# Reordering casts, low parts and sums on ScalarE and VectorE in a hybrid decoder layer

## The chip, the cores and the metric

The kernel runs on one core of a Trainium2 chip. The metric is the device time of one execution in microseconds (us), lower is better. The engines are named as in the profile: PE (TensorE, matmuls), DVE (VectorE), ACT (ScalarE), POOL (GpSimd) and SP (SyncE, which here only issues DMAs). Each engine runs its own instructions in order and waits for others through semaphores.

## The reference

One decoder layer on a sequence of 512 tokens with 1024 channels, all in float32:

```
u = rms_norm(x);  proj = u @ w_in                      # q | k | v | GLU inputs | two gates
q = rms_norm(q)*hd**-0.5;  k = rms_norm(k)             # 16 query heads, 4 key/value heads, hd 64
attn = sliding_window_attention(q, k, v, sinks, bias) @ w_attn_o     # window 128, blocks of 128
conv = silu(layer_norm(depthwise_conv31(a*sigmoid(gate)) + b)) @ w_conv_out
x = x + (sigmoid(gate_a)*attn + sigmoid(gate_c)*conv) @ w_out
x = x + square(relu(rms_norm(x) @ w_ff1)) @ w_ff2      # 4096 hidden channels
```

## The kernel before, in words

**Precision by pieces.** Each float32 matrix is split into a high part (a cast to fp32r, on ScalarE) and a low part (the difference, by a subtraction on VectorE or GpSimd). Each product is three matmuls: high by high, high by low, low by high. A "piece" is one such pair, 128x1024 elements: a 1.0 us cast and a 1.2 us subtraction on VectorE (2.4 us on GpSimd).

**Order written out by hand.** The program is a list of events. `at(pos, fn, args)` puts a step at a position; one unit is about a quarter of a 128x512 output tile, and all events run sorted by position. So the positions fix the order of the instructions on PE, ACT, DVE and POOL. Two steps that share no engine do not care about their mutual order; two that do are executed as listed, and the first that has to wait holds the second. SP's transfers and POOL's are issued in the place of their events too, when what they overwrite has been read.

**Attention part (positions 0 to 152).** TensorE computes the GLU tiles h0 to h7 and the query groups q0 to q3 (order h0 h1 q0 h2 q1 h3 q2 h4 h5 q3 h6 h7), and then the gate tiles, one weight piece per tile, with three buffers each for the high and low parts. A weight piece `u` is split (`split_hi` on ScalarE, `split_lo` on GpSimd) just behind the end of use `u-3`; the raw chunk's buffer is reloaded by `load` after the last split of the chunk. For query group g: `q_step` makes the raw queries, `heads_raw` copies them and squares them on ScalarE, `q_sum` reduces the squares on VectorE, `q_root` and `q_scale` on GpSimd normalise, `q_hi` casts on ScalarE, `q_lo` subtracts on GpSimd, and `q_stage` transposes four times on TensorE (`qtp`, L569) into PSUM and copies on ScalarE (`qT`, L570). In between run the attention units (group g, token block t), six positions apart, starting at `u0`: `score`, `score_max` (DVE), `score_exp` (ACT, L709), `score_norm` (POOL), later `prob` (transposition), `prob_hi`, `prob_lo`, `value` (two matmuls into `op`), `value_low` (ACT copies the lower half of `op` to `osb`, L747) and `value_sum` (DVE adds both halves into `attnT`, L754). `qtp`, `ptp` and `op` share two PSUM slots under one tag; a new tile takes the slot that is free first in the written order and waits for that slot's readers. The convolution's taps (L800, DVE) fill VectorE throughout; some taps run on ScalarE and GpSimd.

**MLP part (from position M0 = 256).** Both MLP products are done in four parts of 1024 hidden channels, each a phase of the first product (even phases 0, 2, 4, 6) and a phase of the second (odd phases 1, 3, 5, 7), 28 positions long each. A phase is one step of Strassen-like block arithmetic with seven products, numbered 1 to 7; `ORDER` gives 1, 2, 7, 6, 5, 4, 3 for phase 0 and 1, 7, 6, 2, 5, 4, 3 for the others. Products share PSUM banks by role: 1, 6, 5, 3 accumulate on one pair of banks (one bank for each token half t), 7 and 4 on a second, 2 on a third; between products of one pair the running value is copied or added out (`c_copy` L1189 on ScalarE, `c_add` L1192 and `row_add` L1180 on VectorE). A product has two halves h, each with a weight piece of its own (`piece_hi` L1142 on ScalarE, `piece_lo` L1145 on VectorE); four piece buffers rotate. Piece 7h1 below is the second half's piece of product 7. The sums of weight blocks that the scheme needs come from accumulating DMAs: after `piece_lo` of one product has read a block, `fetch_add` (L1121, POOL queue) adds another weight block from HBM onto it, and the next product's piece is cast from the result. For product 7 in odd phases that transfer makes the block of product 6. The activations' operands are made by `op_sum` (DVE, L1218 to L1223), `op_hi` (ACT, L1209) and `op_lo` (DVE, L1213, always 0.75 positions behind `op_hi`); P7, P5 and P4 are those of products 7, 5 and 4.

Positions that matter here: `products` of product j in a phase starts at `p = m + 4*j` with `m = M0 + 28*phase`, `piece_hi` is by default at `s = p - 5.9 + 2*h`, `piece_lo` at `s + 0.75`, the DMA at `s + 0.9`.

Of the kernel before, what the change touches and what calls it, by code (L numbers as in the profile page):

```python
# [8 lines left out]
F32 = mybir.dt.float32  # L9
# [3 lines left out]
ALU = mybir.AluOpType  # L13
# [9 lines left out]
HD = 64  # L23
NQ = 16
NG = 4
# [28 lines left out]
def tile_hybrid_block(  # L54
# [23 lines left out]
    ve, se, ge, pe = nc.vector, nc.scalar, nc.gpsimd, nc.tensor  # L78
# [269 lines left out]
    def at(pos, fn, *args):  # L348
        events.append((pos, len(events), fn, args))
# [71 lines left out]
    uses = []  # L421
    chunks = []
    pieces = {}

    def chunk(name, w, c0):
        chunks.append((name, w, c0))
        return len(chunks) - 1
# [99 lines left out]
    qTs, state = {}, {}  # L527
# [29 lines left out]

    def q_lo(g):
        qs = qTs[g][0]
        ge.tensor_tensor(out=qs[:, :, 1, :], in0=state["qraw", g].rearrange("p t (h d) -> p (t h) d", d=HD),  # L560
                         in1=qs[:, :, 0, :].bitcast(F32), op=ALU.subtract)

    def q_stage(g, h):
        qs = qTs[g][0]
# [31 lines left out]
    def q_group(g):  # L596
        nonlocal b
        cq = chunk(f"q{g}", w_in, 256 * g)
        us_ = [use(cq, j, Q_SHAPE, b, b + 8) for j in range(2)]
        for t in range(NT):  # L600
            for i in range(2):
                at(b + 2 * t + i, q_step, g, us_, t, i)
            at(b + 2 * t + 2.8, q_sum, g, t)
        b += 8
        p = b + (4.9 if g < 2 else 1.5)
        at(p, q_root, g)
        at(p, q_scale, g)
        p = max(p + 4.4, 24 * (g - 1) + 42.2)
        at(p, q_hi, g)
        at(p + 0.9, q_lo, g)  # L610

    for part in "h0 h1 q0 h2 q1 h3 q2 h4 h5 q3 h6 h7".split():
        (glu_tile if part[0] == "h" else q_group)(int(part[1]))
    for name, c0, tag, res in (("ta", GLU_END, "gate", ta), ("tc", GA_END, "kT", tcv)):
        at(b + 3.9, gate_tiles, name, tag, res)
        for m in range(0, KD, 2):
            cw = chunk(f"{name}{m // 2}", w_in, c0 + P * m)
            for j in range(2):
                T_tile(use(cw, j, T_SHAPE, b, b + 4), b, f"{name}_{m + j}", u_h, u_l, gate, res, m + j,
                       late=3.3 if name == "tc" and m + j == 0 else 0.2)  # L620
# [43 lines left out]
    last_of = {}  # L664
    for u, (ch, j, _, b0, b1) in enumerate(uses):
        if u >= 3:
            at(uses[u - 3][4] + 0.25, split_hi, u)
            at(uses[u - 3][4] + 0.4, split_lo, u)
            last_of[ch] = uses[u - 3][4] + 0.45
        else:  # L670
            last_of[ch] = -3
    ring = [ch for ch in range(len(chunks)) if chunks[ch][0] != "q1"]
# [84 lines left out]
    for g in range(NG):  # L757
        if g:
            at(24 * g + 40.3, load_bias, g)
        for h, p in enumerate((34.5, 35.6, 40.5, 41.6) if g else (39.6, 40.4, 41.1, 41.8)):  # L760
            at(24 * g + p, q_stage, g, h)
        for t in range(NT):
            u0 = UNIT0 + 6 * (NT * g + t)
            at(u0 + 1.9, sink, g, t)
            for hp in range(2):
                at(u0 + 2.05 + 0.01 * hp, score, g, t, hp)
                at(u0 + 2.65 + 0.8 * hp, score_max, g, t, hp)
                at(u0 + 3.15 + 0.8 * hp, score_exp, g, t, hp)
            at(u0 + 4.9, score_root, g, t)
            at(u0 + 5.0, score_norm, g, t)  # L770
            for kb in range(t == 0, 2):
                at(u0 + 13.05 + 0.01 * kb, prob, g, t, kb)
                at(u0 + 13.5 + 0.6 * kb, prob_hi, g, t, kb)
                at(u0 + 13.8 + 0.6 * kb, prob_lo, g, t, kb)
            at(u0 + 15.4, value, g, t)
            at(u0 + 16.1, value_low, g, t)
            at(u0 + 16.4, value_sum, g, t)

# [166 lines left out]
    for ct in range(KD):  # L947
        p = E + 11.95 + 1.35 * ct
# [14 lines left out]
    M0 = W0 + 32  # L963
# [104 lines left out]
    for t in range(NT):  # L1068
        at(W0 + 16.1 + 0.5 * t, lambda t=t: residual(t, 0, tl["acc"][t]))
        at(W0 + 16.6 + 0.5 * t, residual_square, t, 0)  # L1070
        e = W0 + 20 + 4 * t
# [5 lines left out]
        for half in range(2):  # L1077
            late = (1.2, 0.2, 0, 0)[t]
# [146 lines left out]
    def operands(x, p):  # L1225

        for key, pos in p.items():
            if key[0] == "S":
                at(pos, op_sum, x, int(key[1]))
            else:  # L1230
                at(pos, op_hi, x, int(key[1]))
                at(pos + 0.75, op_lo, x, int(key[1]))
# [18 lines left out]
    def acc_of(ph, prod, t):  # L1251
# [10 lines left out]
    at(M0 + 26, open_a, "O")  # L1262
    at(M0 + 20, open_a, "S")
    operands("x", {"P1": M0 - 3.4, "P2": M0 - 1.7, "S3": M0 + 4.6, "P7": M0 + 5.1, "S2": M0 + 6.6,
                   "P6": M0 + 7.3, "S1": M0 + 10, "P5": M0 + 11.5, "P4": M0 + 15.2, "S4": M0 + 18.6, "P3": M0 + 19.6})
    for h in range(2):
        at(W0 + 1 + 0.1 * h, fetch, 0, 0, 0, 0, h)
        at(W0 + 1.3 + 0.1 * h, fetch, 0, 1, 0, 1, h)
# [2 lines left out]
    for ph in range(PHASES):  # L1271
        m = M0 + 28 * ph
        order = ORDER[ph]
        ff1 = ph % 2 == 0
        h11, ht, h22, h21 = homes(ph)
        if ff1:
            for h in range(2):
                if ph:
                    q1, q3, q2, q4 = m - 4.3 + 2 * h, m - 3.4 + 2 * h, m - 1.0 + 2 * h, m + 8.8 + 1.2 * h
                else:  # L1280
                    q1, q3, q2, q4 = W0 + 7.3 + 4.6 * h, W0 + 18 + 0.9 * h, m + 5.2 + 1.7 * h, m + 10.2 + 0.9 * h
                at(q1, block_sum, h11, h11, ht, h)
                at(q3, block_sum, ht, ht, h22, h)
                at(q2, block_sum, ht, h11, h22, h)
                if ph:
                    at(q4, block_sum, ht, ht, h21, h)
                else:
                    at(m + 7.4 + 2 * h, fetch_add, ph, ht, 1, 0, h)
                at(q4 + 0.1, fetch, ph + 1, h21, 0, 1, h)
                at(q4 + 5, fetch_add, ph + 1, h21, 1, 1, h)  # L1290
        elif ph + 1 < PHASES:
            for h in range(2):
                at(m + 7 + h, fetch, ph + 1, homes(ph - 1)[2], 0, 0, h)
        for j, prod in enumerate(order):
            p = m + 4 * j
            for h in range(2):
                n = 2 * (7 * ph + j) + h
                s, lo = p - 5.9 + 2 * h, 0.75
                if ph == 0 and j < 2:
                    s, lo = ((W0 + 5.6, 0.75), (W0 + 8.2, 0.75), (W0 + 21.8, 1.1), (W0 + 22.6, 4.5))[n]  # L1300
                elif not ff1 and prod == 7:
                    s = m - 2.95 + 3 * h
                elif not ff1 and prod == 6:
                    s = p - 3.4 + 2 * h
                at(s, piece_hi, n, home(ph, prod), h)
                at(s + lo, piece_lo, n, home(ph, prod), h)
                for t in range(2):
                    at(p + 2 * h + t, products, ph, prod, n, h, t)
                d = s + 0.9
                if ff1:  # L1310
                    if prod == 5:
                        at(d, fetch, ph + 1, h11, 0, 0, h)
                    elif prod == 4:
                        at(d, fetch, ph + 1, ht, 1, 0, h)
                elif prod == 1:
                    at(d, fetch_add, ph, h11, 0, 1, h)
                elif prod == 7:
                    at(d, fetch_add, ph, ht, 0, 0, h)
                elif prod == 6:
                    at(d, fetch_add, ph, ht, 1, 0, h)  # L1320
                elif prod == 2:
                    at(d, fetch, ph, h21, 1, 1, h)
                elif ph + 1 < PHASES:
                    at(d, fetch, ph + 1, home(ph, prod), *{5: (0, 1), 4: (1, 1), 3: (1, 0)}[prod], h)
            for t in range(2):
                e = p + 3.1 + t
                if ff1:
                    if prod in (1, 7, 6):
                        at(e, c_copy, {1: 0, 7: 3, 6: 2}[prod], ph, prod, t)
                    elif prod == 3:  # L1330
                        at(e, relu_of, 1, ph, prod, t, -1.0)
                    else:
                        at(e, c_add, {2: 0, 5: 3, 4: 2}[prod], ph, prod, t)
                else:
                    half_t, half_n, minus, store = {1: (0, 0, 0, 0), 7: (1, 1, 1, 0), 6: (1, 0, 0, 0), 2: (0, 0, 0, 1),
                                                    5: (1, 1, 1, 1), 4: (1, 0, 0, 1), 3: (0, 1, 1, 1)}[prod]
                    at(e, row_add, ph, half_t, half_n, prod, t, minus, store)
            if ff1 and prod in (2, 5, 4):
                i, scale = {2: (0, 1.0), 5: (3, -1.0), 4: (2, 1.0)}[prod]
                late = 7.6 if ph == 0 and prod == 2 else 0  # L1340
                at(p + 4.9 + late, relu, i, scale)
                at(p + 5.5 + late, square_of, i)
            elif ff1 and prod == 3:
                at(p + 4.8, square_of, 1)
        if ff1:
            e = {prod: m + 4 * j + 4 for j, prod in enumerate(order)}
            operands("a", {"P1": m + (18.2 if ph else 20.5), "S3": e[4] + 2.2, "P7": e[4] + 2.9, "S2": e[4] + 4.4, "P6": e[4] + 5.1,
                           "P2": e[3] + 7.5, "S1": e[3] + 9.5, "P5": e[3] + 10.3, "P4": e[3] + 13.2,
                           "S4": e[3] + 16, "P3": e[3] + 17})

# [94 lines left out]
```

## Time and profile before

| | |
|---|---|
| median of 3 runs | 764.76 us (764.54 to 764.77) |
| the profiled execution's own time | 764.11 us |
| its span, first to last instruction | 762.3 us |
| TensorE busy | 752.4 us, 99% (weight loads 663.2) |
| VectorE, ScalarE, GpSimd busy | 603.1 (79%), 439.8 (58%), 275.4 us (36%) |
| DMA | 97.48 MB, mean 128 GB/s |
| granted TensorE clock | 1.000 |

How to read the rows that follow. A timeline row has the start, the duration, the engine, the line, the operation, output<-inputs by tile name, shapes and the count of merged instructions; in brackets at the end stands how long the engine was idle before it and what ended that. A row of the waits has who waited for whom, the total, the number of times and the longest. Matmuls are pipelined, so the duration of one is longer than the step from one start to the next, and a wait costs more than the idle time shown.

### The profile page before, as it was taken

Reading aid. Unit: us, or ns where it says so; the run is one execution under the profiler, and the core shown is the slowest. Engines: PE = TensorE matmul, PEld = TensorE weight load, DVE = VectorE, ACT = ScalarE, POOL = GpSimd, SP = SyncE. Lnnn points to the kernel's source line nnn. Section 1 sums busy time; section 2 is a strip of 40 time slices with the busy share of each in tenths; the row PEclk is TensorE's granted clock in tenths of the full one; section 3 lists DMA queues with packets and bytes.
Section 4 is the critical chain, followed back from the end, with each engine's and each line's share of the span. In section 5 each row is a group of like instructions: output and inputs, shape, how many; then the busy total and the mean of one; then the engine's idle time right before and its main releaser. Section 6 shows DMA issues by size and latency. Waiting matters only on the chain.

```text
span 762.3 us, 11662 instructions
## 1 busy us (share of the span) xinstructions
PE 752.4 (99%) x4468; PEld 663.2 (87%) x4468; DVE 603.1 (79%) x926; ACT 439.8 (58%) x697; POOL 275.4 (36%) x215
## 2 busy tenths in 40 slices
PE   9999999999999999999999999999999999999997
PEld 8989989897888888888888899978997899789976
DVE  5466978889878988878435779899879987998696
ACT  7445457756676665349234456854675367636761
POOL 1453978947774566443540002210111011101110
PEclk9999999999999999999999999999999999999999
DMA  7441050312314113431337205983498349833772
GB/s 262 148 158 56 1 164 12 130 56 82 111 57 136 59 55 111 166 110 62 105 110 289 99 28 107 253 193 112 127 232 184 121 116 235 180 134 105 182 156 110
DMA packets 65870, 97.48 MB, mean 128 GB/s; under 512 B 3524, under 2 KB 36340, under 8 KB 65814
## 3 DMA queue, kind: packets, MB, share of 16 engines
q1 hardware_dynamic: 56566, 78.91, 30.5%
q0 software_dynamic: 9248, 17.83, 13.4%
q8 instruction: 35, 0.57, 0.3%
q14 instruction: 21, 0.17, 0.1%
HBM read 94.60 MB, written 2.12 MB: 127 GB/s over the span
## 4 chain that ended last, share of the span: by engine, by line
PE 83%; DVE 5%; ACT 4%; DMA 3%; issue 3%; POOL 2%; POOLq 0%; ACTq 0%; DVEq 0%
PE ps_x L1170 9%; PE ps_z L1175 7%; PE ps_y L1170 5%; PE ps_y L1175 3%; PE ps_x L1175 3%; DMA block<-in_w_ff_dram 3%; PE ps_z L1170 2%; PE ps_ta L498 2%; PE ps_ta L499 2%; PE ps_ta L500 2%; PE ps_tc L500 2%; PE ps_tc L498 2%; PE ps_wo L197 2%; PE ps_wo L199 2%; PE ps_tc L499 2%
## 5 line engine op out<-in xcount | busy, mean ns | idle before, releaser
L1145 DVE TENSOR_TENSOR piecel<-block,pieceh 128x1024 fp32r<-128x1024 f32 x112 | 135.9, 1222 | 30.9 <-ACT pieceh L1142 30.8
L1142 ACT CAST pieceh<-block 128x1024 fp32r<-128x1024 f32 x112 | 116.1, 1049 | 67.2 <-DVE block L1135 20.4
L1121 POOL DMA_DIRECT2D block<-in_w_ff_dram x34 | 41.3, 1238 | 292.3 <-DVE piecel L1145 168.8
L800 DVE SCALAR_TENSOR_TENSOR cv<-h,wcol,cv 128x512 f32<-128x512 f32 x208 | 146.3, 747 | 0.5
L1170 PE MATMUL ps_x<-xSh,pieceh 128*128 128x256 f32 x192 | 53.2, 277 | 1.0 <-ACT c L1189 1.0
L1170 PE MATMUL ps_x<-xSl,pieceh 128*128 128x256 f32 x192 | 53.0, 276 | 0.0
L1170 PE MATMUL ps_x<-xSh,piecel 128*128 128x256 f32 x192 | 53.0, 276 | 0.0
L709 ACT ACTIVATE s<-s,negm 128x257 f32<-128x257 f32 (+1 forms) x64 | 30.4, 478 | 19.5 <-DVE negm L701 19.5
L1175 PE MATMUL ps_z<-piecel,aSh 128*128 128x512 f32 x96 | 37.8, 394 | 1.8 <-DVE piecel L1145 1.8
L1175 PE MATMUL ps_z<-pieceh,aSl 128*128 128x512 f32 x96 | 37.4, 389 | 0.0
L1175 PE MATMUL ps_z<-pieceh,aSh 128*128 128x512 f32 x96 | 37.4, 389 | 0.0
L1135 DVE TENSOR_TENSOR block<-block,block 128x1024 f32<-128x1024 f32 x30 | 36.6, 1223 | 0.7 <-DMA block<-in_w_ff_dram 0.3
L1170 PEld LDWEIGHTS ps_x<-xSh,pieceh 128*128 128x128 f32 x192 | 36.0, 188 | 1.2 <-ACT c L1189 1.2
L197 PE MATMUL ps_q<-wh_q,uTh 128*128 128x256 f32 x128 | 36.5, 285 | 0.0
L199 PE MATMUL ps_q<-wh_q,uTl 128*128 128x256 f32 x128 | 36.2, 283 | 0.0
L198 PE MATMUL ps_q<-wl_q,uTh 128*128 128x256 f32 x128 | 36.2, 283 | 0.0
L1170 PEld LDWEIGHTS ps_x<-xSl,pieceh 128*128 128x128 f32 x192 | 36.0, 188 | 0.0
L1170 PEld LDWEIGHTS ps_x<-xSh,piecel 128*128 128x128 f32 x192 | 36.0, 188 | 0.0
L792 POOL TENSOR_TENSOR side<-side,tap 128x512 f32<-128x512 f32 x24 | 31.1, 1296 | 12.3 <-ACT tap L791 12.2
L1209 ACT CAST aSh<-c 128x1024 fp32r<-128x1024 f32 x16 | 16.8, 1048 | 28.9 <-DVE c L1223 13.2
L718 POOL TENSOR_TENSOR s<-s,r 128x1024 f32<-128x1024 f32 (+1 forms) x16 | 27.0, 1685 | 17.0 <-DVE r L713 14.5
L733 DVE TENSOR_TENSOR pTl<-ptp,pTh 128x512 fp32r<-128x512 f32 x28 | 19.1, 687 | 17.2 <-ACT pTh L729 17.2
(324 smaller groups left out, 2530.5 us busy)
## 6 DMA issues: line engine op xcount, KB each, us to landing
block<-in_w_ff_dram SPq DMA_DIRECT2D x64, 512.0 KB, 5.5
block<-in_w_ff_dram POOLq DMA_DIRECT2D x34, 512.0 KB, 6.3
x<-in_x_dram SPq DMA_DIRECT2D x8, 512.0 KB, 5.2
raw_g<-in_w_in_dram SPq DMA_DIRECT2D x8, 512.0 KB, 4.4
raw_a<-in_w_in_dram SPq DMA_DIRECT2D x8, 512.0 KB, 3.4
raw_q<-in_w_in_dram SPq DMA_DIRECT2D x8, 512.0 KB, 5.4
raw_ta<-in_w_in_dram SPq DMA_DIRECT2D x8, 512.0 KB, 4.4
raw_tc<-in_w_in_dram SPq DMA_DIRECT2D x8, 512.0 KB, 3.4
```

The source lines that it names most:

```text
L197: pe.matmul(ps, ah, wh, start=first, stop=False)
L198: pe.matmul(ps, ah, wl, start=False, stop=False)
L199: pe.matmul(ps, al, wh, start=False, stop=last)
L498: pe.matmul(ps, wh[:, k, :], ah(k), start=(k == 0), stop=False)
L792: ge.tensor_tensor(out=side[ct], in0=side[ct], in1=tap, op=ALU.add)
L800: ve.scalar_tensor_tensor(out=cps[ct], in0=src, scalar=w, in1=cps[ct], op0=ALU.mult, op1=ALU.add)
L1121: ge.dma_start(tl["raw"][buf][:, ks, :], block(ph, i, j)[:, ks, :], accum_op=ALU.add)
L1135: ve.tensor_tensor(out=o, in0=a, in1=b, op=ALU.add)
L1142: se.copy(piece("h", n), tl["raw"][buf][:, 2 * h:2 * h + 2, :])
L1145: ve.tensor_tensor(out=piece("l", n), in0=tl["raw"][buf][:, 2 * h:2 * h + 2, :], in1=piece("h", n).bitcast(F32), op=ALU.subtract)
L1170: pe.matmul(o, b[:, c, w], a[:, k, :], start=(first and c + q + i == 0), stop=(k == 3 and i == 2), skip_group_check=True)
L1175: pe.matmul(acc, a[:, k, w], b[:, c, :], start=(first and c + i == 0), stop=(k == 3 and i == 2), skip_group_check=True)
```

## The change

Nothing is computed differently; the same operations run, some at other places of the order, and one on another engine.

- `q_lo` of group 0 runs on VectorE instead of GpSimd and 2.5 positions later (36.7 instead of 34.2): behind convolution taps and ahead of the reduction `q_sum` of group 1, block 1.
- The splits of two weight pieces come later: the first of query group q2 by 1.75, the second of chunk a1 by 0.65, and with them the reload of a1's raw buffer. They now stand between the copies of group 0's transpositions.
- `value_low` and `value_sum` of blocks t = 0 and 1 in groups 0 to 2 move from u0+16.1 and u0+16.4 to u0+15.93 and u0+15.94: ahead of the second pair of exponentials of the unit two blocks on, and of the query copies at the next group's `q_stage`.
- MLP phase 0: P5's cast moves from M0+11.5 to 12.15 (behind the second copy of product 7 and the cast of piece 5h1), P4's from 15.2 to 16.15 (behind the cast of piece 4h1); the low part of 5h1 moves from 0.75 to 0.85 behind its cast; the cast of piece 4h0 (and its low part and DMA) moves 1.02 later, behind the first copy of product 6.
- All odd phases: the cast of piece 7h1 moves from m+0.05 to m-0.95, and its low part and its accumulating DMA move with it; operand P7 of the second product moves from +2.9 to +3.08. So the cast of 7h1 now stands ahead of P7's cast, and its low part ahead of P7's.

```diff
     def q_lo(g):
         qs = qTs[g][0]
-        ge.tensor_tensor(out=qs[:, :, 1, :], in0=state["qraw", g].rearrange("p t (h d) -> p (t h) d", d=HD),
-                         in1=qs[:, :, 0, :].bitcast(F32), op=ALU.subtract)
+        eng = ge if g else ve
+        eng.tensor_tensor(out=qs[:, :, 1, :], in0=state["qraw", g].rearrange("p t (h d) -> p (t h) d", d=HD),
+                          in1=qs[:, :, 0, :].bitcast(F32), op=ALU.subtract)
...
         at(p, q_hi, g)
-        at(p + 0.9, q_lo, g)
+        at(p + (0.9 if g else 3.4), q_lo, g)
...
         if u >= 3:
-            at(uses[u - 3][4] + 0.25, split_hi, u)
-            at(uses[u - 3][4] + 0.4, split_lo, u)
-            last_of[ch] = uses[u - 3][4] + 0.45
+            late = {("q2", 0): 1.75, ("a1", 1): 0.65}.get((chunks[ch][0], j), 0)
+            at(uses[u - 3][4] + 0.25 + late, split_hi, u)
+            at(uses[u - 3][4] + 0.4 + late, split_lo, u)
+            last_of[ch] = uses[u - 3][4] + 0.45 + late
...
-            at(u0 + 16.1, value_low, g, t)
-            at(u0 + 16.4, value_sum, g, t)
+            ahead = t < 2 and g + 1 < NG
+            at(u0 + (15.93 if ahead else 16.1), value_low, g, t)
+            at(u0 + (15.94 if ahead else 16.4), value_sum, g, t)
...
-                   "P6": M0 + 7.3, "S1": M0 + 10, "P5": M0 + 11.5, "P4": M0 + 15.2, "S4": M0 + 18.6, "P3": M0 + 19.6})
+                   "P6": M0 + 7.3, "S1": M0 + 10, "P5": M0 + 12.15, "P4": M0 + 16.15, "S4": M0 + 18.6, "P3": M0 + 19.6})
...
                 s, lo = p - 5.9 + 2 * h, 0.75
                 if ph == 0 and j < 2:
                     s, lo = ((W0 + 5.6, 0.75), (W0 + 8.2, 0.75), (W0 + 21.8, 1.1), (W0 + 22.6, 4.5))[n]
+                elif ph == 0 and (prod, h) == (5, 1):
+                    lo = 0.85
+                elif ph == 0 and (prod, h) == (4, 0):
+                    s = p - 4.88
                 elif not ff1 and prod == 7:
-                    s = m - 2.95 + 3 * h
+                    s = m - 2.95 + 2 * h
...
-            operands("a", {"P1": m + (18.2 if ph else 20.5), "S3": e[4] + 2.2, "P7": e[4] + 2.9, "S2": e[4] + 4.4, "P6": e[4] + 5.1,
+            operands("a", {"P1": m + (18.2 if ph else 20.5), "S3": e[4] + 2.2, "P7": e[4] + 3.08, "S2": e[4] + 4.4, "P6": e[4] + 5.1,
```

## The prediction

> **What bounds the kernel now.** I read the page's first part, then TensorE's waits, then the timeline of each engine at each of those waits.
>
> ```profile
> PE 752.4 (99%) x4468; PEld 663.2 (87%) x4468; DVE 603.1 (79%) x926; ACT 439.8 (58%) x697; POOL 275.4 (36%) x215
> ```
>
> TensorE bounds the whole span. Only its waits can be shortened, because the edit removes no matmul. Its list of waits is short; the entries that the edit can touch are:
>
> ```profile
> PE ps_z L1175 <- DVE piecel L1145: 1.8, 4, 0.6
> PE ps_x L1170 <- ACT c L1189: 1.0, 1, 1.0
> PE qtp L569 <- POOL qs L560: 0.7, 1, 0.7
> PE qtp L569 <- ACT wh_ta L462: 0.6, 1, 0.6
> PE qtp L569 <- ACT qT L570: 0.4, 1, 0.4
> ```
>
> These are idle times. The lost time is longer, since matmuls overlap: it is the step from start to start less the usual step. From the chain and TensorE's timeline:
>
> ```profile
> 505.72 5.44 PE ps_x L1175 x24
> 97.12 0.28 PE L199 MATMUL ps_q<-wh_q,uTl 128*128 128x256 f32 x1
> 98.13 0.55 PE L569 MATMUL qtp<-ident_r,qs 128*128 128x128 f32 x4 [0.73 <-POOL qs L560]
> 470.56 0.28 PE L1170 MATMUL ps_x<-xSh,piecel 128*128 128x256 f32 x1
> 471.84 0.39 PE L1170 MATMUL ps_x<-xSh,pieceh 128*128 128x256 f32 x1 [1.00 <-ACT c L1189]
> 501.96 0.39 PE L1175 MATMUL ps_z<-pieceh,aSh 128*128 128x512 f32 x1
> 502.94 0.50 PE L1175 MATMUL ps_z<-piecel,aSh 128*128 128x512 f32 x1 [0.59 <-DVE piecel L1145]
> 503.27 0.40 PE L1175 MATMUL ps_z<-pieceh,aSl 128*128 128x512 f32 x1
> ```
>
> A 512-column matmul steps by 5.44/24 = 0.23 us, a 256-column one by about half, 0.12. So at 97.12 the first query transposition loses 98.13-97.12-0.12 = 0.89 us. At 470.56 product 5 of MLP phase 0 loses 1.28-0.12 = 1.16, and about 0.1 more in a slow first step. At 501.96 product 6 of phase 1 loses 0.98-0.23 = 0.75 and 0.10 in the step after: 0.85. That wait comes four times, once in each second-MLP phase: 1.8 idle + 4 x 0.16 overlap + 4 x 0.10 = 2.84, of which 2.0 is in phases 3, 5 and 7. The other two transpositions lose 0.6+0.16 = 0.8 and 0.4+0.16 = 0.6. The edit is aimed at 0.89+1.27+2.84+0.8+0.6 = 6.4 us; that is the ceiling.
>
> **Second MLP product (four places, expected 2.0 from phases 3, 5 and 7).** Phase 1, by ScalarE, VectorE and GpSimd:
>
> ```profile
> 489.93 1.05 ACT L1209 CAST aSh<-c 128x1024 fp32r<-128x1024 f32 x1 [1.47 <-DVE c L1218]
> 491.37 1.04 ACT L1142 CAST pieceh<-block 128x1024 fp32r<-128x1024 f32 x1
> 495.50 1.05 ACT L1142 CAST pieceh<-block 128x1024 fp32r<-128x1024 f32 x1 [0.56 <-DMA block<-in_w_ff_dram]
> 500.57 1.05 ACT L1142 CAST pieceh<-block 128x1024 fp32r<-128x1024 f32 x1 [2.80 <-DMA block<-in_w_ff_dram]
> 491.01 1.23 DVE L1213 TENSOR_TENSOR aSl<-c,aSh 128x1024 fp32r<-128x1024 f32 x1 [1.11 <-ACT aSh L1209]
> 493.41 1.22 DVE L1145 TENSOR_TENSOR piecel<-block,pieceh 128x1024 fp32r<-128x1024 f32 x1
> 501.65 1.23 DVE L1145 TENSOR_TENSOR piecel<-block,pieceh 128x1024 fp32r<-128x1024 f32 x1 [1.40 <-ACT pieceh L1142]
> 489.12 1.20 POOL L1121 DMA_DIRECT2D block<-in_w_ff_dram  x1 [0.95 <-DVE piecel L1145]
> 495.05 1.22 POOL L1121 DMA_DIRECT2D block<-in_w_ff_dram  x1 [4.73 <-DVE piecel L1145]
> ```
>
> Backwards from the stall: piece 6h1 gets its low part at 501.65-502.88, its cast at 500.57, its accumulating DMA 495.05-500.57 (5.5 us), and that DMA had to wait for piece 7h1's low part, 493.41-494.63. The edit moves the cast of 7h1 one position up, ahead of operand P7's cast (489.93), and its low part ahead of P7's (491.01). ScalarE idles 1.47 just before P7's cast, VectorE 1.11 before P7's low part; a cast takes 1.05, a low part 1.22. The cast is held only until the product before has finished with the piece's buffer, which is where phase 1 starts: product 6 at 499.24 (its 12 matmuls before 501.96) less two products of 5.44 gives 488.4. So the cast runs about 488.6-489.7 and P7's is not delayed. The low part runs 489.8-491.0 and P7's low part starts at 491.0 as before. The DMA is issued at about 491.4 instead of 495.05. It follows the one issued at 489.12 on the same queue, which landed at 495.50; allowing each 2.5 us more, it lands by 498.0. Cast and low part then need 2.3 us: 500.3, against a need at 501.96+0.23 = 502.19. The stall goes with about 2 us to spare. What is late next: nothing that TensorE waited for in this phase. P7's own move (2.9 to 3.08) only keeps it behind the cast. I take the full 2.0 in phases 3, 5, 7; ends: 0 and 2.0.
>
> **Phases 0 and 1 together (expected 1.3).** Phase 0, ScalarE, VectorE, GpSimd, and the block tiles' time from issue to landing in 460 to 500 us:
>
> ```profile
> 467.87 1.05 ACT L1209 CAST xSh<-cx 128x1024 fp32r<-128x1024 f32 x1 [2.11 <-DVE cx L1220]
> 471.20 0.58 ACT L1189 COPY c<-ps_x 128x512 f32<-128x512 f32 x1
> 473.11 1.06 ACT L1142 CAST pieceh<-block 128x1024 fp32r<-128x1024 f32 x1
> 472.76 1.22 DVE L1213 TENSOR_TENSOR xOl<-cx,xOh 128x1024 fp32r<-128x1024 f32 x1
> 466.96 3.70 POOL L1121 DMA_DIRECT2D block<-in_w_ff_dram  x3 [3.22 <-DVE piecel L1145]
> DMA to landing us min/median/max: 5.5/6.5/13.2
> ```
>
> Product 5 waits until ScalarE has copied product 6 out of its bank (471.20). In front of that copy stood, in order, P5's cast (467.87, itself idle 2.11 for a sum on VectorE), a copy, and the casts of pieces 5h1 and 4h0. The edit lets the copy (0.58) and the cast of 5h1 (1.05) run inside those 2.11, and puts the copy out ahead of 4h0. P5's cast ends at 468.92 as before; token half 0 of product 6 is done one 1.36 us quarter before the product's end, about 469.5; the copy ends at 470.1, before TensorE wants the bank (470.67). The 1.27 go. Price: P4's cast now stands behind the cast of 4h1, which waits for the transfer issued at 466.96. That landed between 466.96+5.5 = 472.5 and 473.11 (its cast then started without idling). The cast of 4h1 ends 473.5 to 474.2, P4's one later, and its low part, two low parts of 1.15 on, at 475.9 to 476.5, formerly 473.98. Product 4 wants it at 470.67+5.44+0.1 = 476.2: 0 to 0.4 come back, I take 0.25. Behind it both engines run some 0.6 us later than before while TensorE is 1.0 earlier, so phase 1 begins with 1.6 us less slack: piece 6h0, behind the transfer that landed at 495.50, would be late for product 6 by about 0.6 (estimate: low part 498.8 against 498.2). So 1.27+0.85-0.25-0.6 = 1.3; ends 2.1 (nothing comes back) and 0.
>
> **Query low part on VectorE (0.8).** GpSimd, VectorE; then a subtraction with two SBUF inputs beside a GpSimd subtraction:
>
> ```profile
> 93.31 2.41 POOL L466 TENSOR_TENSOR wl_g<-raw_g,wh_g 128x1024 fp32r<-128x1024 f32 x1
> 95.69 2.38 POOL L560 TENSOR_TENSOR qs<-qraw,qs 128x1024 fp32r<-128x1024 f32 x1
> 93.80 0.41 DVE L282 TENSOR_REDUCE ssq<-sq 128x4 f32<-128x256 f32 x1
> 107.41 0.35 DVE L701 CUSTOM_DVE_ANT_0 s<-sp,bias,rb_sink 128x128 f32<-128x128 f32 x1 [3.99 <-PE sp L694]
> 313.40 2.84 POOL L466 TENSOR_TENSOR wl_wo<-raw_wo,wh_wo 128x1024 fp32r<-128x1024 f32 x1 [1.80 <-ACT wh_wo L462]
> 314.56 2.76 DVE L862 TENSOR_TENSOR aTl<-attnT,aTh 128x1024 fp32r<-128x1024 f32 x1
> ```
>
> GpSimd reaches it at 95.69 and ends at 98.07, so the transposition starts at 98.13. VectorE would start at 93.80, ahead of that reduction. Alone it costs 1.22, but it has the shape and neighbour of the subtraction at 314.56: that took 2.76 and ended 1.09 after GpSimd's. So it ends near 95.72+1.09 = 96.8, before 97.24. VectorE's later work slides by 3.0 us, which the 3.99 idle before 107.41 takes; through the sums of squares ScalarE's square and the first query copy slide by about 1 us, for which I charge 0.1. 0.89-0.1 = 0.8; ends 0 and 0.9. The later casts of the third query group and of a1 (1.75 and 0.65) only let the query copies pass; their consumers are four and more units off, so zero. Their loads follow the low parts by under 1 us: zero.
>
> The Trainium skill (SBUF — State Buffer, Who interferes with whom) says that a VectorE instruction with two SBUF inputs and a GpSimd one that reads SBUF hold the second read port in turn, each for a whole instruction, by order of issue. The pair at 313.40 and 314.56 agrees. By it alone the sum would stay 5.4 or, if GpSimd's next instruction is counted as issued first, be 4.6.
>
> **Sums of the value products (1.3).** ScalarE and VectorE:
>
> ```profile
> 176.43 0.58 ACT L747 COPY osb<-op 64x512 f32<-64x512 f32 x1
> 177.04 0.59 ACT L570 CAST qT<-qtp 128x512 fp32r<-128x512 f32 x1
> 177.05 0.85 DVE L754 TENSOR_TENSOR attnT<-op,osb 64x256 f32<-64x256 f32 x2 [0.70 <-ACT osb L747]
> 187.57 0.51 ACT L709 ACTIVATE s<-s,negm 128x257 f32<-128x257 f32 x1 [1.90 <-DVE negm L701]
> 189.30 0.85 DVE L754 TENSOR_TENSOR attnT<-op,osb 64x256 f32<-64x256 f32 x2
> ```
>
> The transposition at 190.29 takes the PSUM slot of the value product; its slot is free when the sum at 189.30 ends (190.15). The copy before it moves into the 1.90 idle before 187.57; the sum ends 188.7 to 189.4, and TensorE comes at 189.5: 0.8 won; ends 0.6 and 0.8. The one near 177 waited for the query copy at 177.04-177.63, whose slot it took over. ScalarE is full there, so that copy comes 0.1 earlier at most; but with the sum now ending at about 177.1 the value product's slot is the first to be free. I take 0.5; ends 0.1 and 0.6. The same move in groups 0 and 2 meets no wait today, and lies within idle time of both engines: zero.
>
> **Sum.** 2.0+1.3+0.8+1.3 = 5.4 us. The profiled execution took 764.11 (span 762.3): 758.7, span 756.9. The median shown, 764.76, is 0.65 above it, so 759.4.
>
> **Rivals.** (1) Everything goes and nothing comes back: 6.4 us, 758.4. For it: no other wait of TensorE is near; against: VectorE and ScalarE in phase 0 have little idle left. (2) GpSimd's next instruction takes the port at 95.72 before VectorE: low part at 98.2, as late as today; 760.2. The pair at 313.40 had no GpSimd successor before 322.03, so the trace does not decide. (3) The earlier accumulating DMA shares the engines with the one issued at 489.12 and delays it, so that 6h0 is late instead of 6h1. If two 5.5 us transfers shared equally from 491.4 on, the first would slip from 495.50 by up to 4 us; from 1.5 on the stall is back. All of the 2.0 and 0.3 of the 1.3 are lost: 764.76-3.1 = 761.7. Against it: three such DMAs already run 2.2 to 2.3 us apart and the last took 6.4 instead of 5.5. The Trainium skill (DMA: Bandwidth & Descriptors, Issuing engines are not separate DMA queues) speaks for it: all transfers interleave on the same 16 engines; the 6.4 agrees only mildly. (4) Slower: the transfer issued at 466.96 takes the 13.2 that its neighbour took. P4's cast, now behind 4h1's, slips by 480.2-472.8 = 7.4, product 4 with it: 764.8-5.4+7.4 = 766.8. It decides from a landing 5.4 us later than today. Against it: it is the second of the burst, and what precedes it is unchanged. (5) No change: VectorE and ScalarE set the pace of splitting weights, so each wait that goes is met again at the next product of its stage: 764.8. Against it: between the waits shown TensorE runs whole products at the bare 5.44, and VectorE is busy 79% of the time.
>
> **How the numbers follow.** Forecast 0.55 (758.7 to 760.5), rival 1 0.12, rival 2 0.13, rival 3 0.10, rival 4 0.05, rival 5 0.05. What can be told from no change here is 0.2%, 1.5 us. Faster: the first four, 0.90; same 0.05; slower 0.05. The range 757.9 to 761.8 holds the first four cases, with 0.5 below rival 1 for small waits that I left out.
>
> **What would show it.** TensorE's waits lose the entry of L560, the four of ps_z L1175 and the 1.0 of ps_x; the DMA of 7h1 is issued within 2.5 us of the one before; the query low part is a VectorE instruction of about 2.8 us; the transposition near 177 starts within 0.1 of its step. Wrong would be a new wait of product 4 for xOl, of product 6 for its first piece, or the first transposition still at 98.

## The result and the profile after

The changed kernel takes 759.2 us (median of four runs, 758.84 to 759.90) against 764.65 (764.52 to 764.77) for the kernel before on the same chip: ratio 0.993, 95% interval 0.9913 to 0.9947. The forecast was 759.4, and it is right in total. Its terms are not all right, and the two profiled executions differ by less than the medians: the one shown before took 764.11 us, the one shown after 759.90 (span 758.1), the slowest of its four. So the profiled pair has 4.2 us between its spans where the forecast's sum is 5.4. One execution among all below is left out of every comparison: the profiled one of the changed kernel without part 0's edits, which ran at a granted clock of 0.655 and took 1068 us.

First the page's busy times of the changed kernel:

```profile
PE 751.4 (99%) x4468; PEld 663.5 (88%) x4468; DVE 605.8 (80%) x927; ACT 441.1 (58%) x697; POOL 273.3 (36%) x214
```

VectorE has the one instruction more that GpSimd has less. From the list of waits, the entries of TensorE's matmuls behind the start-up, and one of its weight loads (waited for: us in total, times, longest):

```profile
PE ps_y L1173 <- DVE xOl L1216: 1.1, 1, 1.1
PE ps_y L1173 <- ACT xOh L1212: 0.2, 1, 0.2
...
PEld mu_ps L878 <- DVE ta L628: 0.5, 1, 0.5
```

All waits that the edit was aimed at are gone: the one for the query low part, the four ps_z, the 1.0 of ps_x, the other two transpositions. One wait is new and one is longer: product 4 of MLP phase 0 waits for operand P4 (xOh, then xOl), and the first weight load of the statistics, near 321, waits 0.5 where it waited 0.2 before:

```profile
PEld mu_ps L875 <- DVE ta L627: 0.2, 1, 0.2
```

(Lines of the changed file are higher by 1 to 3.) TensorE's timeline at the places of the prediction:

```profile
96.67 0.28 PE L199 MATMUL ps_q<-wh_q,uTl 128*128 128x256 f32 x1
96.79 0.45 PE L570 MATMUL qtp<-ident_r,qs 128*128 128x128 f32 x4
...
175.32 0.40 PE L500 MATMUL ps_g<-uTh,wl_g 128*128 128x512 f32 x1
175.56 0.46 PE L570 MATMUL qtp<-ident_r,qs 128*128 128x128 f32 x4
...
187.10 0.40 PE L500 MATMUL ps_g<-uTh,wl_g 128*128 128x512 f32 x1
187.34 0.45 PE L570 MATMUL qtp<-ident_r,qs 128*128 128x128 f32 x4
...
468.00 0.28 PE L1173 MATMUL ps_x<-xSh,piecel 128*128 128x256 f32 x1
468.11 0.28 PE L1173 MATMUL ps_x<-xSh,pieceh 128*128 128x256 f32 x1
...
473.44 0.28 PE L1173 MATMUL ps_x<-xSh,piecel 128*128 128x256 f32 x1
473.90 0.38 PE L1173 MATMUL ps_y<-xOh,pieceh 128*128 128x256 f32 x1 [0.19 <-ACT xOh L1212]
475.35 0.39 PE L1173 MATMUL ps_y<-xOl,pieceh 128*128 128x256 f32 x1 [1.07 <-DVE xOl L1216]
475.57 0.28 PE L1173 MATMUL ps_y<-xOh,piecel 128*128 128x256 f32 x1
...
497.55 0.39 PE L1178 MATMUL ps_z<-pieceh,aSh 128*128 128x512 f32 x1
497.90 0.50 PE L1178 MATMUL ps_z<-piecel,aSh 128*128 128x512 f32 x1
...
500.52 0.39 PE L1178 MATMUL ps_z<-pieceh,aSh 128*128 128x512 f32 x1
500.76 0.50 PE L1178 MATMUL ps_z<-piecel,aSh 128*128 128x512 f32 x1
```

The three transpositions now start one usual step (0.12, 0.24, 0.24) behind the matmul before them. Product 5 starts 0.11 after product 6's last matmul instead of 1.28. But product 4 starts 0.46 after product 5's last and needs 1.45 and 0.22 for its first two steps, 1.8 lost in all. Product 6 of phase 1 starts its second matmul 0.35 after the first (0.12 lost, for 6h0), and at 6h1, where 0.75 was lost, the step is a plain 0.24.

TensorE runs the same 4468 matmuls in the same order in both traces, so each can be paired with its twin. The difference of their start times, from 40 us on, shows where time was won (negative) and lost:

| place | predicted | profiled pair | second profiled run of the changed kernel |
|---|---|---|---|
| query transpositions 98 and 102 | -0.8 | -1.05 | -1.09 |
| transpositions 177 and 190 | -1.3 | -1.46 | -1.44 |
| statistics, 321 | 0 | +0.24 | +0.25 |
| phase 0: product 5 | -1.27 | -1.26 | -1.28 |
| phase 0: product 4 | +0.25 | +1.80 | +1.05 |
| phase 1: 6h0, late | +0.6 | +0.23 | +0.62 |
| phase 1: 6h1 | -0.85 | -0.71 | -0.71 |
| phases 3, 5, 7: 6h1 | -2.0 | -2.02 | -2.02 |

(Left out: the first 40 us, which differ by up to 0.6 from one run to another; 0.15 in small steps lost before phase 0 in both runs; and 0.4 behind the wait of product 4 in the first run alone, where from 476 to 487 us each step of a 256-column matmul takes 0.118 us instead of 0.113, at a granted clock of 1.00; why, no run shows.) Everything stands near its prediction but product 4 and the statistics.

### The profile page after: what moved, and what is told of

It is laid out like the page before. It is cut to its first block, busy times and chain, and to the rows that moved or that the text cites. A ratio compares the mean times of both kernels' runs of the same rounds, so it can differ in the third digit from the quotient of the medians.

```text
span 758.1 us, 11662 instructions
## 1 busy us (share of the span) xinstructions
PE 751.4 (99%) x4468; PEld 663.5 (88%) x4468; DVE 605.8 (80%) x927; ACT 441.1 (58%) x697; POOL 273.3 (36%) x214
## 4 chain that ended last, share of the span: by engine, by line
PE 94%; DVE 3%; DMA 1%; issue 1%; ACT 0%; POOL 0%; DVEq 0%; POOLq 0%; ACTq 0%
PE ps_z L1178 12%; PE ps_x L1173 10%; PE ps_y L1178 6%; PE ps_y L1173 5%; PE ps_x L1178 3%; PE ps_z L1173 2%; PE ps_g L498 2%; PE ps_q L197 2%; PE ps_q L198 2%; PE ps_q L199 2%; PE ps_a L498 2%; PE ps_ta L498 2%; PE ps_g L500 2%; PE ps_a L500 2%; PE ps_g L499 2%; PE ps_ta L500 2%
```

## The experiments

Twelve runs, one of them the changed kernel once more. Ratios are against the kernel before, on the same chip, with 95% intervals. That kernel's medians beside the experiments, on three chips, were 765.46, 765.21 and 765.26, somewhat above the 764.65 of the first comparison; so ratios are compared.

**The odd MLP phases alone.** The kernel before with these two lines changed:

```
-                    s = m - 2.95 + 3 * h
+                    s = m - 2.95 + 2 * h
...
-  "P7": e[4] + 2.9,
+  "P7": e[4] + 3.08,
```

> The kernel before with the edit of the odd MLP phases alone. Theory (the stall at product 6 is the accumulating transfer's late issue behind piece 7h1, in each of the four phases): the four waits of 0.6 go, 2.0 in phases 3, 5 and 7 and 0.85 in phase 1, 764.65 - 2.85 = 761.8. Rival (the stall of phase 1 went in the changed kernel only because TensorE came later there): phase 1 keeps its wait, 762.6. Rival (the earlier transfer delays 6h0): 764 or more.

Measured: 761.68, ratio 0.9948 (0.9936 to 0.9961), 3.0 to 4.9 us. The four waits of ps_z are gone in its list; against the profiled run before, the pairs give -0.91 in phase 1 and -0.74, -0.62, -0.70 in the others, 2.97. So phase 1 gains by itself, without part 0. That the ratio says more is explained by the next run.

**The attention part alone** (the query low part on VectorE, the two later splits, the earlier sums):

> The kernel before with the attention part's edits alone (query low part on VectorE, two later splits, earlier sums). Theory: 0.95 at the first query transposition and 0.2 at the third, 0.65 near 177, 0.8 near 190, all lasting to the end: 764.65 - 2.6 = 762.05. Rival (the new wait of the first statistics product near 321 is caused by this edit and gives back 0.3 every time): 762.35. Rival (VectorE, now with 3 us more work, gives back more in later stages): 763 or more.

Measured: 762.95, ratio 0.997 (0.9959 to 0.9982). The pairs give -1.11 at 98 and 102, -1.43 at 177 and 190, +0.28 at 321, as in the changed kernel. Its waits show something else:

```profile
PE ps_z L1178 <- DVE piecel L1148: 2.9, 4, 0.8
```

These phases were not touched, and yet wait 2.9 instead of the 1.8 of the profiled run before. The same entry is 3.0 in three of the kernels below that leave these phases' transfers where they were, and 3.7 in five waits in a fourth. By the pairs, this kernel and two more that leave these phases alone (the low part alone and the sums alone, below) lose 1.1, 1.8 and 2.1 us more there than the trace of before. So the 1.8 is low, and what the odd phases' edit removes is commonly 1 to 2 us more than the 2.84 that the trace of before showed. Whether it is the execution or the chip that made it low is open.

**MLP part 0 alone** (P5 and P4 moved, 4h0's cast earlier, 5h1's low part later):

> The kernel before with the edits of MLP part 0 alone. Theory (product 5's wait of 1.3 goes, but product 4 waits for operand P4, whose cast stands behind that of 4h1 and so behind its transfer): 1.3 won, 1.4 to 1.8 given back, and what is left makes 6h0 no earlier: 764.6 to 765.2, and a wait of product 4 for xOl of 1 us or more in the profile. The prediction's sizes (0.25 given back at product 4, 0.6 in phase 1): 764.2, and that wait under 0.3.

Measured: 766.35, ratio 1.0015 (1.0006 to 1.0024): slower by 0.5 to 1.8, more than expected. ScalarE, GpSimd and TensorE:

```profile
472.46 1.05 ACT L1142 CAST pieceh<-block 128x1024 fp32r<-128x1024 f32 x1 [1.39 <-DMA block<-in_w_ff_dram]
473.42 1.04 ACT L1209 CAST xOh<-cx 128x1024 fp32r<-128x1024 f32 x1
...
466.49 1.20 POOL L1121 DMA_DIRECT2D block<-in_w_ff_dram  x1 [3.22 <-DVE piecel L1145]
...
475.64 0.28 PE L1170 MATMUL ps_y<-xOh,pieceh 128*128 128x256 f32 x1
475.97 0.39 PE L1170 MATMUL ps_y<-xOl,pieceh 128*128 128x256 f32 x1
476.19 0.28 PE L1170 MATMUL ps_y<-xOh,piecel 128*128 128x256 f32 x1
```

Here the transfer takes 6.0 us from issue to the cast that waits for it, and product 4 loses 0.32, within the 0 to 0.4 of the prediction. My expectation, drawn from the one trace after, was wrong on this. What makes this kernel slower comes later: TensorE reaches phase 1 about 1.0 earlier, and there loses 0.98 at 6h0 and, against the trace of before, 0.92 more at 6h1, whose DMA still stands behind 7h1's old place. (At 6h1 three kernels that leave phases 0 and 1 alone lose 0.1 to 0.9 more than that trace too, so not all of the 0.92 belongs to the edit.) What was won in phase 0 was lost again in phase 1.

**P4 ahead of 4h1.** The changed kernel with

```
+                elif ph == 0 and (prod, h) == (4, 1):
+                    s = p - 3.8
```

> The changed kernel with one thing more: in part 0 the cast and low part of piece 4h1 stand behind those of operand P4 instead of ahead. Theory (P4's cast waits only because it stands behind a cast that waits for a transfer): product 4's waits for xOh and xOl go, 1.4 to 1.8, 757.5 to 757.8; 4h1's low part, two to three us after its landing at 472, is still ahead of its need at 476.3. Rival (the transfers of part 0 set the pace, and the time is met again at piece 4h1 or at product 3's pieces): 759.2, with a wait for a piece in place of that for xOl.

Measured: 758.6, ratio 0.9913 (0.99 to 0.9927). The waits for xOh and xOl are gone; ScalarE:

```profile
469.30 1.06 ACT L1212 CAST xOh<-cx 128x1024 fp32r<-128x1024 f32 x1
471.83 1.05 ACT L1145 CAST pieceh<-block 128x1024 fp32r<-128x1024 f32 x1 [1.48 <-DMA block<-in_w_ff_dram]
```

The order alone did it: the transfer of 4h1 was late here too (6.92 from issue to landing), and nothing waited for it. But of the 1.78 won against the trace after, 0.25 came back at product 7 of phase 1, whose operand's low part was late, and 0.45 at 6h0, where 0.68 is lost: 1.1 is left of it between the two traces, and in the ratios the kernel cannot be told from the changed kernel. The rival was half right: part of it is met again at a piece behind a transfer, though later than it said, in phase 1.

**The changed kernel once more.**

> The changed kernel once more, to see how far the landing of part 0's second accumulating transfer and the wait of product 4 vary. Theory (the transfer of 4h1 takes 5.9 us in some executions and 7 to 7.4 in others, and product 4 pays what is over about 6): 4h1 lands 5.9 to 7.4 after its issue, and the wait for xOl is that time less about 6.1; 0.993 of the time before. Rival (in the changed kernel it is always 7 or more, since something in it is issued beside it): 7.0 to 7.4, wait of 1 to 1.4.

Measured: 758.75 (758.64 to 759.41), ratio 0.9917 (0.9904 to 0.9931). ScalarE, GpSimd and TensorE:

```profile
471.36 1.05 ACT L1145 CAST pieceh<-block 128x1024 fp32r<-128x1024 f32 x1 [2.13 <-DMA block<-in_w_ff_dram]
...
464.67 2.44 POOL L1124 DMA_DIRECT2D block<-in_w_ff_dram  x2 [3.23 <-DVE piecel L1148]
...
474.86 0.39 PE L1173 MATMUL ps_y<-xOl,pieceh 128*128 128x256 f32 x1 [0.77 <-DVE xOl L1216]
```

4h1's transfer took 6.62 from issue to landing, and product 4 lost 1.05. Over the four traces with P4 behind 4h1, landing and loss go together: 5.89 and 0.32 (part 0 alone), 6.31 and 0.74 (the last experiment), 6.62 and 1.05, 7.37 and 1.80. Loss = transfer - 5.57 in each. So the rival, always 7 or more in the changed kernel, falls. In nine other traces, of kernels that do not put P4 behind 4h1, the same transfer took 5.89 to 6.92, so the spread does not belong to the change, though the longest, 7.37, was seen in it. In all thirteen the issues beside it stand at nearly the same distances (the next on its queue 0.73 to 0.74 us behind it, SyncE's first load 1.98 to 1.99), so these do not make the spread; what does is open.

**The changed kernel without part 0's edits.**

> The changed kernel without the edits of MLP part 0. Theory (these edits win 1.25 at product 5 and give back 0.3 to 1.8 at product 4 and 0.3 to 1 at 6h0): the same as the changed kernel within 0.8 us, rather faster; product 5's wait of 1.0 is back, those of product 4 for xOh and xOl and of product 6 for its first piece are gone. The prediction's sizes (1.27 won, 0.85 given back): 0.4 slower than the changed kernel. Rival (the part's net gain is the whole 1.3): 1.3 slower.

Measured: 758.83 (758.69 to 759.50, four executions), ratio 0.9918 (0.9905 to 0.9932), the same as the changed kernel's 758.75 within 0.1. Its only trace is that of the execution at 1068 us, so its waits could not be read; the rest of the expectation stays open. In the second trace part 0's edits cost 0.4 at the places listed (-1.28 + 1.05 + 0.62), so that they are worth nothing agrees within half a microsecond. The rival's 1.3 would have put it at 760.1, above all four.

**Row sums ahead of P6.** The changed kernel with P4 ahead of 4h1, and in the second MLP phases both sums of product 1's rows at p + 1.6:

> The changed kernel with 4h1's cast and low part behind P4's, and in each second MLP phase the two sums of product 1's rows ahead of P6's low part instead of behind it, so that 6h0's low part starts as its cast ends. Theory (of the 0.68 that product 6 of phase 1 waits for 6h0 there, 0.25 is VectorE's order and the rest the transfer's landing): 0.25 under the kernel with the first edit alone, 758.3, 0.992 x the time before less 0.5. Rival (P6's low part, 0.13 later, or the sums that wait for TensorE hold VectorE up): 758.6 or more.

Measured: 777.03, ratio 1.0153 (1.0139 to 1.0167). That position stands ahead of the second half of product 1 in the program's order, so the sum takes the product before that half is in (the half is left out of the output), and TensorE, about to write the bank, waits for the sum in the middle of product 1: 4.6 us in phase 1 and 2.9 in each of phases 3, 5 and 7. By the pairs the loss there is larger in three of the four: 6.3, 4.8, 4.8 and 3.2. Behind the waits of phases 1, 3 and 5 the granted clock is 0.50 for 3.4 us (491.8 to 495.2, 573.7 to 577.1, 655.6 to 659.0), and a 512-column matmul steps by 0.43 instead of 0.23; behind the wait of phase 7, as long as those of 3 and 5, it stays at 1.00. It says nothing on 6h0.

**Early cast, low part and DMA at their old places.** The kernel before with the two lines of the odd phases, and 7h1's low part and accumulating DMA kept back:

```
+                    s, lo = m - 2.95 + 2 * h, 0.75 + h
...
+                d = s + 0.9 if lo < 0.9 or ff1 else s + lo + 0.1
```

> The kernel before with piece 7h1's cast early, as in the change, in the second MLP phases, but its low part and with it the accumulating transfer at their old places. Theory (what counts is when the low part lets go of the block, since the transfer waits for that): no gain, 0.999 to 1.001 of the time before, the four waits of product 6 stay at 0.6 or more. Rival (the early cast relieves ScalarE and the low part moves by itself): 1.0 or more faster.

Measured: 766.6, ratio 1.0017 (1.0008 to 1.0026). GpSimd's issues in phase 1, and TensorE's wait:

```profile
489.70 1.20 POOL L1121 DMA_DIRECT2D block<-in_w_ff_dram  x1 [0.95 <-DVE piecel L1145]
495.88 1.22 POOL L1121 DMA_DIRECT2D block<-in_w_ff_dram  x1 [4.97 <-ACT aSh L1209]
```

```profile
PE ps_z L1175 <- DVE piecel L1145: 3.0, 4, 0.8
```

The cast ran at 488.95, 2.4 us earlier than in the trace before, but the DMA was issued 6.2 after the one ahead of it (before: 5.9), and all four waits are there. The cast's place wins nothing by itself; what the edit buys is the DMA's issue. The kernel is even 0.6 to 2.0 us slower than the one before, more than I expected; whether the slightly later DMA does that, no run separates.

**The query low part on VectorE, and nothing else.**

> The kernel before with the first query low part on VectorE, and nothing else (no later splits, no earlier sums). Theory: 0.89 won at the first transposition; the 0.2 of the third transposition, near 102, comes only with the later splits and stays lost; the 0.27 that the first statistics product loses near 321 comes with the one instruction more in VectorE's stream and shows here too: 0.6 faster, 0.999 of the time before. Rival (that 0.27 belongs to the sums): 0.9 faster and no wait near 321. Rival (the third transposition gains by the low part's move): 0.85 to 1.1 faster.

Measured: 766.41, ratio 1.0015 (1.0006 to 1.0024): slower, against all three expectations. The pairs give -0.89 at the first transposition and +1.37 at the third; TensorE's wait and ScalarE's order there:

```profile
PE qtp L570 <- ACT qT L571: 1.9, 2, 1.4
```

```profile
98.85 0.38 ACT L281 ACTIVATE sq<-ps_q 128x256 f32<-128x256 f32 x1 [1.04 <-DVE ssq L282]
99.13 0.58 ACT L571 CAST qT<-qtp 128x512 fp32r<-128x512 f32 x1
99.59 1.06 ACT L462 CAST wh_a<-raw_a 128x1024 fp32r<-128x1024 f32 x1
100.55 1.05 ACT L462 CAST wh_q<-raw_q 128x1024 fp32r<-128x1024 f32 x1
101.49 1.08 ACT L571 CAST qT<-qtp 128x512 fp32r<-128x512 f32 x2
```

VectorE's three microseconds delay the sum of squares and with it ScalarE's square; the next query copies then stand behind two weight casts and come at 101.49, too late. In the changed kernel the later splits let the copies pass, and TensorE does not wait. The wait of the statistics is here too (+0.26).

**The sums of the value products alone.**

> The kernel before with the earlier low parts and sums of the value products alone. Theory: the transposition near 190 wins 0.8 (its slot is the value product's, free earlier), that near 177 wins 0.6 (it gets that slot instead of the query copy's), 1.4 in all, 0.998 of the time before, and no wait near 321. Rival (the 0.6 near 177 comes from the later split of a1 or from the low part's move): 0.8.

Measured: 763.82, ratio 0.9981 (0.9972 to 0.9989). -0.60 at 177, -0.78 at 190, nothing at 321: the theory's 1.4, and the 0.6 needs neither the split of a1 nor the low part.

**Second row sum behind 6h0's low part.** The changed kernel with P4 ahead of 4h1, and

```
-                e = p + 3.1 + t
+                e = p + 3.1 + t * (2.3 if not ff1 and prod == 1 else 1)
```

> The changed kernel with 4h1's cast and low part behind P4's, and in the second MLP phases the second row sum of product 1 behind 6h0's low part instead of ahead of it, so that this low part starts as its cast ends. Theory (0.25 of the 0.68 that product 6 of phase 1 waits for 6h0 is VectorE's order): the wait falls to about 0.4, 0.25 under the kernel with the first edit alone (0.991 of the time before). Rival (the second half of product 6 then waits for that row sum, whose bank it takes): a new wait of about 0.3 for it in each of the four phases, 1 slower.

Measured: 758.44 (758.34 to 758.52), ratio 0.9907 (0.9894 to 0.9921), the lowest median here. The wait at 6h0 falls by 0.5, but at 6h1 0.6 comes back. ScalarE, VectorE and TensorE there:

```profile
495.96 1.06 ACT L1145 CAST pieceh<-block 128x1024 fp32r<-128x1024 f32 x1 [0.51 <-DMA block<-in_w_ff_dram]
...
496.27 1.22 DVE L1148 TENSOR_TENSOR piecel<-block,pieceh 128x1024 fp32r<-128x1024 f32 x1
497.41 0.68 DVE L1183 TENSOR_TENSOR x<-x,ps_y 128x512 f32<-128x512 f32 x1
498.01 1.22 DVE L1148 TENSOR_TENSOR piecel<-block,pieceh 128x1024 fp32r<-128x1024 f32 x1
...
499.28 0.50 PE L1178 MATMUL ps_z<-piecel,aSh 128*128 128x512 f32 x1 [0.45 <-DVE piecel L1148]
```

6h1's cast ends at 497.02, but its low part starts at 498.01, behind another piece's low part and a row sum. It is VectorE's order once more, and neither of the two expectations: the wait moved to the next piece. The sum behind 6h0 was not waited for. Its four runs (758.34 to 758.52) lie below every run of the two kernels at 758.75 (lowest 758.64). Against the kernel with P4 ahead of 4h1 alone (758.27 to 759.16, on another chip) no gain is shown; the intervals overlap.

**The low part asks before GpSimd.** The changed kernel with 3.4 replaced by 3.0 in the query low part's place:

> The changed kernel with VectorE's query low part one instruction earlier, so that it is ready at about 92.8, while GpSimd's sum of 91.7 to 93 still runs and before GpSimd's next subtraction starts. Theory (the two engines take turns, by order of asking): the low part gets its turn when that sum ends, ends near 94.1 instead of 96.4, and GpSimd's subtraction ends near 96.4 instead of 95.3. Rival (GpSimd's next instruction goes first): the low part takes 3.6 and ends at 96.4 as now. The time: within 0.3 of the changed kernel either way.

Measured: 758.75, ratio 0.9913 (0.9899 to 0.9926). First the changed kernel's VectorE and GpSimd, then this one's:

```profile
93.34 3.06 DVE L561 TENSOR_TENSOR qs<-qraw,qs 128x1024 fp32r<-128x1024 f32 x1
...
92.91 2.42 POOL L466 TENSOR_TENSOR wl_g<-raw_g,wh_g 128x1024 fp32r<-128x1024 f32 x1
```

```profile
93.10 1.23 DVE L561 TENSOR_TENSOR qs<-qraw,qs 128x1024 fp32r<-128x1024 f32 x1
...
93.20 3.40 POOL L466 TENSOR_TENSOR wl_g<-raw_g,wh_g 128x1024 fp32r<-128x1024 f32 x1
```

The same instruction takes 3.06 when GpSimd's subtraction is already running and 1.23 when it comes first, and then GpSimd's takes 3.40 instead of 2.42. The theory of turns holds, the rival does not. The time is unchanged: either way the low part is ready (96.40 or 94.33) before TensorE is.

## Why the prediction was right, and where it was wrong

**Second MLP product: right, in mechanism and in size.** 2.02 against 2.0 in phases 3, 5 and 7, 0.71 of 0.85 in phase 1. ScalarE, VectorE and GpSimd of the changed kernel:

```profile
488.03 1.03 ACT L1145 CAST pieceh<-block 128x1024 fp32r<-128x1024 f32 x1
...
489.47 1.22 DVE L1148 TENSOR_TENSOR piecel<-block,pieceh 128x1024 fp32r<-128x1024 f32 x1
...
488.78 1.21 POOL L1124 DMA_DIRECT2D block<-in_w_ff_dram  x1 [0.95 <-DVE piecel L1148]
491.12 1.22 POOL L1124 DMA_DIRECT2D block<-in_w_ff_dram  x1 [1.12 <-DVE piecel L1148]
...
497.63 1.05 ACT L1145 CAST pieceh<-block 128x1024 fp32r<-128x1024 f32 x1 [0.61 <-DMA block<-in_w_ff_dram]
```

The DMA is issued 2.34 behind the one before it (predicted: within 2.5) and its data are cast at 497.63 (predicted landing: by 498.0). Rival 3, two transfers sharing the engines so that 6h0 comes late, fell: the one issued at 488.78 took 6.17, against 6.3 in the trace before, where nothing was issued behind it for 5.9 us. The kernel with the early cast and the late DMA shows that it is the issue that counts. What the trace of before could not show is that its 1.8 of waits is low for that kernel.

**Phases 0 and 1: the mis-sized term.** The predicted gain was 1.3, the ends 2.1 and 0. In the profiled pair it is nothing (-1.26 + 1.80 + 0.23 - 0.71 = +0.06, with the longer steps behind the wait a loss of about 0.4), in the second trace a gain of 0.3, and by the comparison with and without part 0's edits that part is worth nothing within half a microsecond. The failed step is the landing of 4h1: "between 466.96+5.5 = 472.5 and 473.11", that is 5.5 to 6.15 from its issue. In the changed kernel's first trace it took 7.37, and the casts of 4h1 and P4 started late behind it:

```profile
471.85 1.05 ACT L1145 CAST pieceh<-block 128x1024 fp32r<-128x1024 f32 x1 [2.88 <-DMA block<-in_w_ff_dram]
472.81 1.04 ACT L1212 CAST xOh<-cx 128x1024 fp32r<-128x1024 f32 x1
...
464.41 3.70 POOL L1124 DMA_DIRECT2D block<-in_w_ff_dram  x3 [3.23 <-DVE piecel L1148]
```

The mechanism behind it, P4's cast held by the cast ahead of it, was the right one and its arithmetic holds (0.32 lost with 5.89). The term was mis-sized: 0.25 was taken, and 0.32 to 1.80 came. The bound came from one transfer in one execution, where it held (5.89); its neighbours in the same burst took 10.65 and 13.2, and the same transfer varies from 5.89 to 7.37. I had that risk only as a rival of its own, with the whole 7.4 and a chance of 0.05, not as a spread of the main case. The lower end of the gain, 0, was met in the first trace.

**Query low part: the sum right, the attribution wrong.** 0.8 was predicted and 1.05 to 1.09 came, 3.06 for the low part against the 2.76 forecast, ending at 96.40 against 96.8. But "the first query copy slides by about 1 us, for which I charge 0.1" and "later casts ... zero" hold only together: without the later splits the slide costs 1.37, and the move by itself loses. The prediction said that the splits let the query copies pass, but gave that no price; it is what the 0.8 rests on.

**Sums: right.** 0.59 and 0.79 against 0.5 and 0.8, and alone 0.60 and 0.78.

**Not foreseen: the wait of the statistics,** 0.25. Ahead of one sum on VectorE in the changed kernel, whose inputs are ready when the tap before it ends, VectorE is idle 0.46 us:

```profile
318.98 0.69 DVE L807 TENSOR_TENSOR cv<-side,cv 128x512 f32<-128x512 f32 x1 [0.46 <-DVE cv L803]
```

It is 0.46 in eight traces with the query low part on VectorE, that of the kernel with this move alone among them, and 0.10 in all five without. So it comes with the move, which gives VectorE's program one instruction more; by what way, no run here shows.

**Why the total was right nevertheless.** In the profiled pair the terms miss by 1.2 in sum. The medians make it good: the kernel before runs 0.55 above its profiled execution, the changed one 0.7 below its own. That is luck: nothing in the prediction foresaw it.

## What to carry to other kernels

Before moving an instruction to another place of an engine's queue, look at what will stand in front of it there: behind one that waits for a transfer, it pays that transfer's spread, which one trace does not show. Where a stall ends with a DMA, look for what held its issue; here an earlier cast with the DMA issued as late as before gained nothing. Edits that each remove a wait are not worth their sum: one was a loss without its companion (the low part without the later splits), another a loss until a later stage had been relieved (part 0).

## What was not expected of the hardware

Accumulating DMAs on GpSimd's queue, 512 KB each: where phase 1 issues one 5.9 to 6.2 us behind the one ahead, it takes 5.5 to 5.85 us; with four issued 2.15 to 2.35 us apart, in the changed kernel, they land 2.56, 2.63 and 2.66 apart, in order, and take 5.45, 5.69, 6.17 and 6.50. In this stretch they queue, and a later one hardly slows an earlier one. In phase 0, with SyncE's loads beside them, three issued 0.74 and 1.20 apart take 7.37, 11.23 and 14.08, and land in order too. The Trainium skill (DMA: Bandwidth & Descriptors, Issuing engines are not separate DMA queues) says that transfers run on the same 16 engines and interleave, whatever engine started them. It says so of transfers from several engines; these share one queue, and there the traces show little of it.

The order of asking decides between VectorE and GpSimd: 1.23 and 3.40 us one way, 3.06 and 2.42 the other, for the same two subtractions. The Trainium skill (SBUF — State Buffer, Who interferes with whom) says that the shared port pair is an exclusive lock; both orders agree with it.
